# Overlapping the stages of a second block by halves of x, on one core

## The chip, the cores and the metric

One NeuronCore of a Trainium2 chip runs the whole program. The metric is the device time of one execution in microseconds, as a median over runs. All data is float32; weights stream from HBM.

## The reference, cut to what matters

256 tokens with 1024 channels go through two blocks of two layers each. The first block (token mixers and a mixture of experts) is not changed. The second block is, for layer i:

```python
for i in range(2):
    h = h + 0.5 * swiglu(rms_norm(h, ffn1_norm[i]), wg1[i], wu1[i], wd1[i])   # 1024 -> 2816 -> 1024
    hn = rms_norm(h, mix_norm[i])
    h = h + (rglru_mixer(hn, ...) if i == 0 else pool_mixer(hn, w, b, scale))
    h = h + 0.5 * swiglu(rms_norm(h, ffn2_norm[i]), wg2[i], wu2[i], wd2[i])
    gate = sigmoid(rms_norm(h, ple_norm[i]) @ ple_w_gate[i])
    h = h + gate * (p[i] @ ple_w_proj[i])
return rms_norm(h, final_norm)
```

`swiglu(x) = (silu(x @ wg) * (x @ wu)) @ wd`. `rglru_mixer` projects to 2 x 1280 channels, convolves, computes gates, runs a linear recurrence over the tokens, multiplies by a gelu branch and projects back (`lru_out`). `pool_mixer` takes, for each of four groups of 256 channels, trailing means minus the token, a 256 x 256 map, and returns `(y + b) * scale`.

## The kernel before, in words

x lies in SBUF as two token tiles of 128 x 1024. A product in float32 is made of three matmuls on pairs hi + lo (`mm3`, L324 to L326): a weight of 1 MB comes by a DMA that SyncE issues (`raw`, L275), ScalarE rounds it to `hi` (L308) and VectorE subtracts to `lo` (L309), in four pieces of 128 x 512. `halves_of` (L288) hands out a pair and begins the split of the weight that follows. Weights, pairs and large tiles live in 17 slots of 8 KiB a partition; `phase(n)` says how many of them a stage keeps, and loads run ahead as far as the others go (`pump`).

Each stage of the second block begins with `scaled_T` (L401): 16 transposes of x (`tr`, L397), ScalarE's copy times the gain to `Th` (L411), VectorE's remainder `Tl` (L412). The row norm is a factor that comes in after the products, so `rms_col` runs beside them. The stages:

- `ffn` (L1197): 11 chunks of 256 hidden channels. A chunk is 96 matmuls of 256 columns (`fg`, gate and up) and, one chunk later, 24 of 512 columns onto four accumulators (`acc`, `out_mm` L1247). At the end VectorE adds the four accumulators to x (L1245), and only then do the next stage's transposes start.
- `lru` (L1258): ten products `li`, and between them convolution, gates, two groups of five recurrences on VectorE (L1357) whose inputs GpSimd multiplies (L1356), GpSimd's multiplications by the gelu branch (L1366), and five weights `lru_out` onto `acc`.
- `pool` (L1410): a norm of the rows (`xn`, square and a chain of small VectorE operations), 16 products `pu` with the means' matrix, copies `uT`, 16 products `py`. Then VectorE adds the bias (`pt`, L1432), GpSimd multiplies by the scale (L1434), VectorE adds to x (L1436).
- `ple` (L1439): first p's projection, `pp`, 24 matmuls of 512 columns, with a load and a split of its own (`pT`, `pTh`, `pTl`, weight `ple_p`), copied to `pv`; then transposes, four products `pg`, sigmoid, multiplication by `pv`, addition to x. `ple_final` (L1477) is the last one with the final norm.

The order on each engine is made by a scheduler from the program's order and its estimates, and is fixed when the program is built; each engine then works through its own list in order. PSUM has four banks for `ps` and four for `acc` here.

Of the kernel before, what the change touches and what calls it, by code (L numbers as in the profile page):

```python
# [200 lines left out]
def v2(t):  # L201
    return t.rearrange("p (t n) -> p t n", t=2)


# [1 line left out]
class Prog:  # L206
    def __init__(self, tc, A, off, out, order=None, stop=None):
        """order: the weights' tiles as the program asks for them; None to find it (in self.asked)."""
# [12 lines left out]
    def area(self, psum, tmp):  # L221
        """PSUM banks and small tiles by tag, for a part of the program."""
# [17 lines left out]
    # slots of 8 KiB a partition, given out in the order of the program  # L240
# [47 lines left out]
    def halves_of(self, *key):  # L288
        """hi and lo of a weight; those of the weight that follows are begun before this one's products."""
# [38 lines left out]
    def tok_mm(self, bank, aT, w, t, o=None):  # L328
        """bank[:, o or t] = tokens of tile t x 256 columns of w"""
# [7 lines left out]
    def col_mm(self, bank, w, aT, j):  # L337
        """bank[:, j] = columns j of w x 256 tokens"""
# [7 lines left out]
    def rsqrt(self, ss, n, c):  # L346
        """(ss + c)^-1/2 for [128, n]: a first guess from the exponent's half, a step of third order and one of Newton's."""
# [7 lines left out]
        # y (15/8 - 5/4 w + 3/8 w^2), w = x y^2  # L355
# [15 lines left out]
    def rstd(self, xt, junk=None):  # L371
        """1/sqrt(sum over the row + n eps) for both token tiles; sqrt(n) is left to the caller."""
# [17 lines left out]
    def transposed(self, rows, evac, tags=("ps",) * 4):  # L390
        """rows [128, 2, 1024] -> banks [128, 2 channel tiles, 256 tokens] for evac(k0, bank)."""
# [9 lines left out]
    def scaled_T(self, rows, g, alloc=None):  # L401
        """hi, lo of the transposed rows times the gain column."""
# [14 lines left out]
    def rms_col(self, xt):  # L417
        """1/rms of the rows, [128, 2]."""
# [5 lines left out]
    def rms_row(self, col):  # L424
        """the same along the free axis on every partition, [128, 256]."""
# [9 lines left out]
    def ada(self, l, part, tag="ada"):  # L435
        """part: of shift, scale and gate of the first norm (0 to 2) and of the second (3 to 5)."""
# [1179 lines left out]
```

## Time and profile before

| | |
|---|---|
| median of three runs | 2588.95 us (2579.15 to 2589.79) |
| profiled execution | span 2577.8 us, mean granted TensorE clock 0.925 |
| PE busy | 2253.0 us (87%) |
| VectorE (DVE), ScalarE (ACT), GpSimd (POOL) busy | 1121.9, 796.9, 117.4 us |
| HBM read | 663.20 MB, mean 258 GB/s |
| second block | from about 1578 us to the end |

The profile gives the span of the profiled execution from its first to its last instruction; no other time of that execution is shown. A stage that keeps the PE busy for its whole width is limited by the PE, whatever the other engines' shares are; where the PE is idle, the wait that ends last tells what the stage hangs on. The PE clock is given as a share of full speed (2.4 GHz); half of it is the lower level.

### The profile page before, as it was taken

To read this page: it belongs to the slowest core of one execution; us is meant where nothing else is said; L and a number is where in the kernel's file an instruction comes from. 1 tells how busy PE (TensorE), PEld (TensorE's weight loads), DVE (VectorE), ACT (ScalarE), POOL (GpSimd) and SP (SyncE) were. 2 spreads that over 40 slices of the span, in tenths; PEclk is the share of its full clock that TensorE was granted. 3 is DMA by queue.
4 is the path that set the end of the run, shared out by engine and by line. 5 is a ranking of instruction groups with operands and counts; after the bars stand their busy time and mean duration, and the time that the engine had idled before them with its cause. 6 is when DMAs were issued, how large, how long until landed. Compare 5 with 4: busy or idle time off the path is not lost.

```text
span 2577.8 us, 37968 instructions
## 1 busy us (share of the span) xinstructions
PE 2253.0 (87%) x15658; PEld 1601.2 (62%) x15658; DVE 1121.9 (44%) x2582; ACT 796.9 (31%) x1550; POOL 117.4 (5%) x120
## 2 busy tenths in 40 slices
PE   6999998987878799976666668999899999998997
PEld 4876784322222287742222225999889989988997
DVE  4656563111111476520101105557675566556555
ACT  3244443000000235320000003443764455434444
POOL 0100011000000020010000000000400000000000
PEclk9999798999999999996777778999999999999999
DMA  8365145999999923489999999553365544553540
GB/s 359 144 245 208 55 150 219 417 420 420 420 420 419 381 70 114 166 366 420 419 419 419 419 419 370 190 181 125 125 229 189 188 172 176 180 208 135 189 166 19
DMA packets 92797, 666.72 MB, mean 259 GB/s; under 512 B 10304, under 2 KB 10816, under 8 KB 12496
## 3 DMA queue, kind: packets, MB, share of 16 engines
q1 hardware_dynamic: 92624, 664.29, 65.6%
q8 instruction: 123, 2.02, 0.3%
q14 instruction: 50, 0.41, 0.0%
HBM read 663.20 MB, written 1.05 MB: 258 GB/s over the span
## 4 chain that ended last, share of the span: by engine, by line
PE 37%; DMA 16%; DVE 3%; ACT 1%; issue 1%; POOL 0%; ACTq 0%; SPq 0%; DVEq 0%; POOLq 0%
PE fg L324 7%; PE fg L325 7%; PE fg L326 7%; DMA raw<-in_e_down_dram 6%; DMA raw<-in_e_up_dram 5%; DMA raw<-in_e_gate_dram 5%; PE acc L326 3%; PE acc L324 3%; PE acc L325 3%; PE ri L1339 1%; DVE lo L309 1%; PE pg L324 0%; PE pg L325 0%; PE pg L326 0%; PE li L325 0%
## 5 line engine op out<-in xcount | busy, mean ns | idle before, releaser
L308 ACT CAST hi<-raw 128x512 fp32r<-128x512 f32 x748 | 412.1, 617 | 408.7 <-DVE lo L309 186.2
L309 DVE TENSOR_TENSOR lo<-raw,hi 128x512 fp32r<-128x512 f32 x748 | 479.6, 691 | 132.9 <-PE acc L325 53.9
L324 PE MATMUL fg<-Th,hi 128*128 128x256 f32 x1408 | 402.1, 286 | 6.3 <-DVE Tl L412 6.3
L325 PE MATMUL fg<-Th,lo 128*128 128x256 f32 x1408 | 401.2, 285 | 0.0
L326 PE MATMUL fg<-Tl,hi 128*128 128x256 f32 x1408 | 400.7, 285 | 0.0
L1133 PE MATMUL eu<-raw,XG 128*32 128x256 f32 (+1 forms) x1536 | 216.9, 548 | 73.8 <-DMA raw<-in_e_up_dram 73.8
L324 PEld LDWEIGHTS fg<-Th,hi 128*128 128x128 f32 x1408 | 273.3, 194 | 8.5 <-DVE Tl L412 7.1
L325 PEld LDWEIGHTS fg<-Th,lo 128*128 128x128 f32 x1408 | 273.3, 194 | 1.4
L326 PEld LDWEIGHTS fg<-Tl,hi 128*128 128x128 f32 x1408 | 272.9, 194 | 0.0
L1133 PE MATMUL eg<-raw,XG 128*32 128x256 f32 (+1 forms) x1536 | 207.7, 522 | 60.1 <-DMA raw<-in_e_gate_dram 60.0
L1133 PE MATMUL ed<-raw,hTs 128*32 128x256 f32 (+1 forms) x1536 | 209.4, 530 | 52.3 <-DMA raw<-in_e_down_dram 51.8
L1144 DVE TENSOR_TENSOR hid<-sg,eu 128x512 f32<-128x512 f32 (+1 forms) x32 | 17.7, 554 | 514.6 <-issue 335.8
L1133 PEld LDWEIGHTS eu<-raw,XG 128*32 128x32 f32 (+1 forms) x1536 | 69.0, 136 | 216.9 <-DMA raw<-in_e_up_dram 116.8
L1165 DVE TENSOR_TENSOR osb<-ed,g 32x512 f32<-32x512 f32 (+1 forms) x128 | 70.9, 554 | 279.1 <-PE ed L1133 277.5
L1133 PEld LDWEIGHTS eg<-raw,XG 128*32 128x32 f32 (+1 forms) x1536 | 68.2, 133 | 199.6 <-DMA raw<-in_e_gate_dram 98.7
L1133 PEld LDWEIGHTS ed<-raw,hTs 128*32 128x32 f32 (+1 forms) x1536 | 66.0, 133 | 179.7 <-DMA raw<-in_e_down_dram 103.4
L1141 ACT ACTIVATE sg<-eg 128x512 f32<-128x512 f32 (+1 forms) x32 | 15.7, 490 | 507.1 <-PE eg L1133 507.0
L324 PE MATMUL acc<-hi,fhh 128*128 128x512 f32 x352 | 137.4, 390 | 0.0
L325 PE MATMUL acc<-hi,fhl 128*128 128x512 f32 x352 | 137.4, 390 | 0.0
L324 PE MATMUL wi<-hi,hTh 128*128 128x256 f32 x448 | 134.6, 301 | 3.0 <-DVE lo L309 2.2
L326 PE MATMUL acc<-lo,fhh 128*128 128x512 f32 x352 | 136.9, 389 | 0.0
L326 PE MATMUL wi<-lo,hTh 128*128 128x256 f32 x448 | 132.3, 296 | 2.5 <-DVE lo L309 2.4
(319 smaller groups left out, 3415.7 us busy)
## 6 DMA issues: line engine op xcount, KB each, us to landing
raw<-in_e_gate_dram SPq DMA_DIRECT2D x128, 1024.0 KB, 19.9
raw<-in_e_up_dram SPq DMA_DIRECT2D x128, 1024.0 KB, 19.9
raw<-in_e_down_dram SPq DMA_DIRECT2D x128, 1024.0 KB, 19.9
raw<-in_ada_dram SPq DMA_DIRECT2D x48, 1024.0 KB, 6.9
raw<-in_ffn_g_dram SPq DMA_DIRECT2D x44, 1024.0 KB, 4.9
raw<-in_ffn_u_dram SPq DMA_DIRECT2D x44, 1024.0 KB, 4.9
raw<-in_ffn_d_dram SPq DMA_DIRECT2D x44, 1024.0 KB, 4.8
raw<-in_w_in_dram SPq DMA_DIRECT2D x18, 1024.0 KB, 19.9
```

Of the source, the lines that this page charges most:

```text
L308: self.nc.scalar.copy(hi[:, c], src[:, c])
L309: self.nc.vector.tensor_tensor(lo[:, c], src[:, c], hi[:, c].bitcast(F32), ALU.subtract)
L324: mm(out, ah, bh, start=first, stop=False)
L325: mm(out, al, bh, start=False, stop=False)
L326: mm(out, ah, bl, start=False, stop=last)
L1133: nc.tensor.matmul(p[M * c:M * c + M, 0:N], lhs(k), v2(w)[:, kk, c * N:c * N + N], start=k == 0, stop=k == 7, tile_position=(0, M * c))
L1141: nc.scalar.activation(sg[:, 0:N], pg[:, 0:N], AF.Silu)
L1144: nc.vector.tensor_tensor(hid[:, 0:N], sg[:, 0:N], pu[:, 0:N], ALU.mult)
L1165: nc.vector.tensor_tensor(ob[r:r + 32, s, c * N:c * N + N], p[q0:q0 + 32, 0:N], g2[r:r + 32, s, c * N:c * N + N], ALU.mult)
L1339: nc.tensor.matmul(b[:, gi * 256:gi * 256 + 256], wt, xc[BLOCKS[n][0]], start=q == 0, stop=q == len(ids) - 1)
```

## The change

The transposed halves of x become a class `Turn`, made two channel tiles at a time by `turn(k0)`, in banks of the `acc` tag. `out_mm` finishes the accumulators of the first 512 channels before those of the second; in the last chunk `between` adds them to x at once, and the next stage's `turn(0)` and `turn(2)` are placed in the middle of the second half. The first products of a stage are made for two weights, on channel tiles 0 to 3 first, then `turn(4)`, `turn(6)`, then tiles 4 to 7. The norm's column waits behind those copies. The pool's scale is multiplied into bias and weights on GpSimd, the bias is added to x on GpSimd, and VectorE adds `py` to x out of PSUM. The projection of p becomes `ple_values`, run as a filler in `lru` (ahead of the last gelu) and in `pool` (between norm and `pu`); `pv` is kept through the second feed-forward, so `phase` is 10 there instead of 9 (12 instead of 11 in `lru`). In the first block only the order of the last combine's four additions changes.

```diff
+class Turn:
+    def turn(self, k0):
...
+        b = p.ps("tr", "acc")
+        xv = v2(p.x)
+        for kk in range(2):
+            for t in range(2):
+                nc.tensor.transpose(b[:, kk * 256 + t * 128:kk * 256 + t * 128 + 128],
+                                    xv[:, t, (k0 + kk) * 128:(k0 + kk + 1) * 128], p.con("ident"))
+        for kk in range(2):
+            k = k0 + kk
+            s, g = b[:, kk * 256:kk * 256 + 256], self.gain[:, k:k + 1]
+            self.act = nc.scalar.activation(self.hi(k), s, AF.Copy, scale=g)
+            self.dve = nc.vector.scalar_tensor_tensor(self.lo(k), s, g, self.hi(k).bitcast(F32), ALU.mult, ALU.subtract)
...
+    def out_mm(self, acc, w, a, first, last, between=None):
+        wh, wl = w
+        for d in range(2):
+            for j, (ah, al) in enumerate(a):
+                for t in range(2):
+                    o = t * 128
+                    q = j * 1024 + d * 512
+                    self.mm3(acc[d][t], ah[:, o:o + 128], al[:, o:o + 128], wh[:, q:q + 512], wl[:, q:q + 512],
+                             first and j == 0, last and j == 1)
+                if between is not None:
+                    between(d, j)
+
+    def residual(self, acc, add, nxt):
+        def between(d, j):
+            if j == 1:
+                for t in range(2):
+                    add(acc[d][t], v2(self.x)[:, t, d * 512:d * 512 + 512], t)
+            if nxt is not None and (d, j) == (1, 0):
+                nxt.turn(0)
+                nxt.turn(2)
+        return between
...
+            ws = [self.halves_of(f"ffn{n}_{m}", i, c) for m in "gu"]
+            bs = [self.ps("fg") for _ in "gu"]
+            T.turn(0)
+            T.turn(2)
+            for b, w in zip(bs, ws):
+                for j in range(2):
+                    if b is bs[1] and j == 1:
+                        T.turn(4)
+                        T.turn(6)
+                    self.col_part(b, w, T, (j,), range(4))
+            for b, w in zip(bs, ws):
+                self.col_part(b, w, T, (0, 1), range(4, 8))
+                self.free(*w)
+                yield b
...
             if c == 0:
-                col = self.rms_col(self.x)
+                with self.behind(T.act), self.behind(T.dve):
+                    col = self.rms_col(self.x)
...
         scan(range(5, NT))
         branch(4)
+        filler()
         gelu(2, 3, 4)
         out(range(4, NT))
...
-    def pool(self):
+    def pool(self, nxt, filler):
         nc = self.nc
-        xn = self.norm_rows(self.x)
...
+        filler()
         mw, pw, brt = self.weight("k_pool"), self.weight("pool_w"), self.weight("brow2")
         br = v2(brt)
+
+        nc.gpsimd.tensor_tensor(br[:, 0], br[:, 0], br[:, 1], ALU.mult)
+        pws = self.big("pws")
+        for gi in range(4):
+            s = br[:, 1, gi * 256:gi * 256 + 256].unsqueeze(1).to_broadcast([128, 2, 256])
+            p2 = lambda a: a[:, gi * 512:gi * 512 + 512].rearrange("p (c n) -> p c n", c=2)
+            nc.gpsimd.tensor_tensor(p2(pws), p2(pw), s, ALU.mult)
...
+            xs = v2(self.x)[:, :, gi * 256:gi * 256 + 256]
+            nc.gpsimd.tensor_tensor(xs, xs, br[:, 0, gi * 256:gi * 256 + 256].unsqueeze(1).to_broadcast([128, 2, 256]), ALU.add)
...
-            tv = self.t2("pt").rearrange("p (t n) -> p t n", t=2)
-            o = gi * 256
-            nc.vector.tensor_tensor(tv, b.rearrange("p (t n) -> p t n", t=2),
-                                    br[:, 0, o:o + 256].unsqueeze(1).to_broadcast([128, 2, 256]), ALU.add)
-            nc.gpsimd.tensor_tensor(tv, tv, br[:, 1, o:o + 256].unsqueeze(1).to_broadcast([128, 2, 256]), ALU.mult)
-            xs = v2(self.x)[:, :, o:o + 256]
-            nc.vector.tensor_tensor(xs, xs, tv, ALU.add)
-        self.free(xn, mw, pw, brt, uTt)
-
-    def ple(self, i):
+            xs = v2(self.x)[:, :, gi * 256:gi * 256 + 256]
+            nc.vector.tensor_tensor(xs, xs, b.rearrange("p (t n) -> p t n", t=2), ALU.add)
+
+        means(0)
+        for gi in range(4):
+            if gi < 3:
+                means(gi + 1)
+            mapped(gi)
+            if gi:
+                nxt.turn(2 * gi - 2)
+        self.free(xn, mw, pw, brt, uTt, pws)
+
+    def ple_values(self, i):
...
+            if nxt is not None and n > 1:
+                nxt.turn(2 * n - 4)
             yield n
-        self.free(*hT, pvt)
...
+        self.free(self.pv)
+        if nxt is not None:
+            nxt.turn(4)
```

How this moves instructions shows at three places. The rows name line, operation, output, inputs and shape; a count stands behind rows that follow each other.

VectorE at the start of the second block's first feed-forward, from the last combine's additions (`x<-x,cb`) on. Before:

```order
L1176 TENSOR_TENSOR x<-x,cb 128x512
L309 TENSOR_TENSOR lo<-raw,hi 128x512
L1176 TENSOR_TENSOR x<-x,cb 128x512 x3
L309 TENSOR_TENSOR lo<-raw,hi 128x512 x3
L412 SCALAR_TENSOR_TENSOR Tl<-tr,cols,Th 128x256 x7
L309 TENSOR_TENSOR lo<-raw,hi 128x512 x2
L412 SCALAR_TENSOR_TENSOR Tl<-tr,cols,Th 128x256
L309 TENSOR_TENSOR lo<-raw,hi 128x512 x6
```

Now:

```order
L1212 TENSOR_TENSOR x<-x,cb 128x512
L345 TENSOR_TENSOR lo<-raw,hi 128x512
L1212 TENSOR_TENSOR x<-x,cb 128x512 x3
L345 TENSOR_TENSOR lo<-raw,hi 128x512 x11
L238 SCALAR_TENSOR_TENSOR T<-tr,cols,T 128x256 x8
L414 SCALAR_TENSOR_TENSOR junk,ss<-x 128x1024
```

Eight more splits, of the second and the third weight, stand ahead of the transposed halves.

VectorE in the recurrent stage, from the second group of five recurrences (`lf<-lf`, x5 before and x1, x4 now) to the additions of the output product. Before:

```order
L1357 SCALAR_TENSOR_TENSOR lf<-lf 128x256 x5
L309 TENSOR_TENSOR lo<-raw,hi 128x512 x3
L1315 TENSOR_TENSOR lf<-li,rrow 128x256 x2
L309 TENSOR_TENSOR ly<-lf,ly 128x256 x6
L309 TENSOR_TENSOR lo<-raw,hi 128x512 x28
```

Now:

```order
L1456 SCALAR_TENSOR_TENSOR lf<-lf 128x256
L1452 SCALAR_TENSOR_TENSOR lf<-q,lf 128x256
L1456 SCALAR_TENSOR_TENSOR lf<-lf 128x256 x4
L345 TENSOR_TENSOR lo<-raw,hi 128x512 x4
L1414 TENSOR_TENSOR lf<-li,rrow 128x256 x2
L345 TENSOR_TENSOR pTl<-pT,pTh 128x512
L345 TENSOR_TENSOR lo<-raw,hi 128x512 x4
L345 TENSOR_TENSOR ly<-lf,ly 128x256 x6
L345 TENSOR_TENSOR lo<-raw,hi 128x512 x28
```

The first four `lo` are now those of `ple_p`, the next four those of the first `lru_out` weight, of which the first piece stood ahead of the recurrences before.

The PE in the pool stage, from `pu` to the first gate product. Before:

```order
L326 MATMUL acc<-lo,fhh 128x512
L1420 MATMUL pu<-raw,xn 128x256 x16
L1428 MATMUL py<-raw,uT 128x256 x16
L397 MATMUL tr<-k_early,x 128x128 x16
L324 MATMUL fg<-Th,hi 128x256
```

Now:

```order
L362 MATMUL pp<-lo,pTh 128x512
L1546 MATMUL pu<-raw,xn 128x256 x8
L1557 MATMUL py<-pws,uT 128x256 x4
L1546 MATMUL pu<-raw,xn 128x256 x4
L1557 MATMUL py<-pws,uT 128x256 x4
L232 MATMUL tr<-k_early,x 128x128 x4
L1546 MATMUL pu<-raw,xn 128x256 x4
L1557 MATMUL py<-pws,uT 128x256 x4
L232 MATMUL tr<-k_early,x 128x128 x4
L1557 MATMUL py<-pws,uT 128x256 x4
L232 MATMUL tr<-k_early,x 128x128 x4
```

The row ahead of `pu` is the last of 24 `pp` now; the means, the maps and the transposes are interleaved, and the last four transposes follow 36 `fg`.

## Rows read from the trace of the kernel before

**Rows 1.** Busy time by stretch: window, width, busy (records) of five engines, clock, DMA.

```profile
1600.00:1765.00 165.00, 165.00 (x1170) 155.73 (x1169) 91.29 (x148) 74.12 (x133) 0.10 (x1) 1.00 0.53 186
```

**Rows 2.** What the PE waits for from 1578 us on: total, times, longest.

```profile
PE fg L324 <- DVE Tl L412: 6.3, 3, 2.3
PE pu L1420 <- issue: 5.5, 1, 5.5
PE acc L326 <- DVE lo L309: 5.0, 1, 5.0
PE li L325 <- DVE lo L309: 4.9, 1, 4.9
...
PE pg L324 <- DVE Tl L412: 3.3, 2, 1.7
```

**Rows 3.** Timeline, pool stage: start, duration, engine, operation, count, idle time before.

```profile
2322.21 8.75 PE L1420 MATMUL pu<-raw,xn 128*128 128x256 f32 x32 [5.54 <-issue]
2330.80 7.07 PE L1428 MATMUL py<-raw,uT 128*128 128x256 f32 x32
2337.71 0.60 PE L397 MATMUL tr<-k_early,x 128*128 128x128 f32 x4
...
2344.72 0.57 PE L324 MATMUL fg<-Th,hi 128*128 128x256 f32 x1
...
2348.72 0.41 PE L325 MATMUL fg<-Th,lo 128*128 128x256 f32 x1
2348.93 0.41 PE L326 MATMUL fg<-Tl,hi 128*128 128x256 f32 x1
...
2349.61 0.28 PE L325 MATMUL fg<-Th,lo 128*128 128x256 f32 x1
2349.73 0.28 PE L326 MATMUL fg<-Tl,hi 128*128 128x256 f32 x1
...
2337.53 2.49 POOL L1434 TENSOR_TENSOR pt<-pt,raw 128x512 f32<-128x512 f32 x2 [1.90 <-DVE pt L1432]
```

**Rows 4.** Timeline, second recurrent wait, on PE, VectorE and GpSimd.

```profile
1863.34 0.40 PE L324 MATMUL acc<-hi,ly 128*128 128x512 f32 x1
...
1864.95 0.39 PE L325 MATMUL acc<-hi,ly 128*128 128x512 f32 x1
1870.36 0.80 PE L326 MATMUL acc<-lo,ly 128*128 128x512 f32 x1 [5.01 <-DVE lo L309]
...
1862.59 5.51 DVE L1357 TENSOR_TENSOR_SCAN lf<-lf 128x256 f32<-128x256 f32 x5 [0.63 <-POOL lf L1356]
1868.03 3.40 DVE L309 TENSOR_TENSOR lo<-raw,hi 128x512 fp32r<-128x512 f32 x3
1871.36 0.74 DVE L1315 TENSOR_TENSOR lf<-li,rrow 128x256 f32<-128x256 f32 x2
...
1866.46 4.43 POOL L1366 TENSOR_TENSOR lf<-lf 128x256 f32<-128x256 f32 x4
```

**Rows 5.** Timeline, start of the second block's first feed-forward.

```profile
1579.95 1.89 DVE L309 TENSOR_TENSOR lo<-raw,hi 128x512 fp32r<-128x512 f32 x3
1581.76 3.01 DVE L412 SCALAR_TENSOR_TENSOR Tl<-tr,cols,Th 128x256 fp32r<-128x256 f32 x7
...
1583.46 0.39 PE L324 MATMUL fg<-Th,hi 128*128 128x256 f32 x1 [2.26 <-DVE Tl L412]
```

**Rows 6.** Timeline, VectorE within a feed-forward loop, GpSimd idle.

```profile
2006.80 2.49 DVE L309 TENSOR_TENSOR lo<-raw,hi 128x512 fp32r<-128x512 f32 x4
```

**Rows 7.** Busy time by stretch at three seams, columns as in Rows 1.

```profile
1772.20:1778.00 5.80, 4.28 (x31) 3.50 (x30) 5.71 (x13) 5.56 (x14) 0.30 (x3) 1.00 0.01 1
...
1898.00:1907.00 9.00, 7.14 (x48) 6.87 (x47) 7.12 (x25) 4.17 (x10) 0.00 (x0) 0.81 0.81 321
...
2122.00:2132.00 10.00, 7.32 (x46) 6.42 (x46) 8.36 (x19) 10.00 (x24) 0.00 (x0) 0.83 0.31 105
```

**Rows 8.** The page's list of DMA issues: count, KB each, us to landing.

```profile
raw<-in_ffn_g_dram SPq DMA_DIRECT2D x44, 1024.0 KB, 4.9
```

More of the change, by code (lines that the diff above doesn't have):

```diff
@@ L1194, in moe, with turner, col_part @@
         self.free(gwb, g2b)
-    def ffn(self, i, n):
+    def turner(self, gain):
+        return Turn(self, gain)
+    def col_part(self, bank, w, T, js, ks):
+        wh, wl = [v8(a) for a in w]
+        mm = self.nc.tensor.matmul
+        for j in js:
+            o = bank[:, j * 256:j * 256 + 256]
+            for k in ks:
+                h, l = T.hi(k), T.lo(k)
+                c = slice(j * 128, j * 128 + 128)
+                mm(o, wh[:, k, c], h, start=k == 0 and j == 0, stop=False, skip_group_check=True)
+                mm(o, wh[:, k, c], l, start=False, stop=False, skip_group_check=True)
+                mm(o, wl[:, k, c], h, start=False, stop=k == 7, skip_group_check=True)
@@ new lines, in tok_part @@
+    def tok_part(self, bank, w, T, t, ks):
+        wh, wl = [v8(a) for a in w]
+        mm = self.nc.tensor.matmul
+        o = bank[:, t * 256:t * 256 + 256]
+        c = slice(t * 128, t * 128 + 128)
+        for k in ks:
+            h, l = T.hi(k)[:, c], T.lo(k)[:, c]
+            mm(o, h, wh[:, k, :], start=k == 0 and t == 0, stop=False, skip_group_check=True)
+            mm(o, l, wh[:, k, :], start=False, stop=False, skip_group_check=True)
+            mm(o, h, wl[:, k, :], start=False, stop=k == 7, skip_group_check=True)
@@ new lines, in accumulators @@
+    def accumulators(self):
+        return [[self.ps("acc", "acc") for _ in range(2)] for _ in range(2)]
+    def out_mm(self, acc, w, a, first, last, between=None):
[9 more added lines that the diff above has]
+                    between(d, j)
@@ L1240, in ffn, with lru @@
         down(NC - 1, prev)
-        self.free(*hT)
-        for d in range(2):
-            for t in range(2):
-                xs = v2(self.x)[:, t, d * 512:d * 512 + 512]
-                nc.vector.scalar_tensor_tensor(xs, acc[t][d], rms["half"][:, t:t + 1], xs, ALU.mult, ALU.add)
-    def out_mm(self, acc, w, a, first, last):
-        wh, wl = w
-        for d in range(2):
-            for j, (ah, al) in enumerate(a):
-                for t in range(2):
-                    o = t * 128
-                    q = j * 1024 + d * 512
-                    self.mm3(acc[t][d], ah[:, o:o + 128], al[:, o:o + 128], wh[:, q:q + 512], wl[:, q:q + 512],
-                             first and j == 0, last and j == 1)
-    def lru(self):
+    def lru(self, T, nxt, filler):
         nc = self.nc
@@ L1296, in product @@
             b = self.ps("li")
-            for j in range(2):
-                self.col_mm(b, w, hT, j)
+            self.col_part(b, w, T, (0, 1), range(8))
             self.free(*w)
@@ L1367, in out @@
                 self.halves(yh[m], yl[m], mu[m])
-        banks = [product(5)]
-        col = self.rms_col(self.x)
-        banks.append(product(6))
+        ws = [self.halves_of("lru_in", c) for c in (5, 6)]
+        banks = [self.ps("li") for _ in range(2)]
+        T.turn(0)
+        T.turn(2)
+        for b, w in zip(banks, ws):
+            for j in range(2):
+                if b is banks[1] and j == 1:
+                    T.turn(4)
+                    T.turn(6)
+                self.col_part(b, w, T, (j,), range(4))
+        for b, w in zip(banks, ws):
+            self.col_part(b, w, T, (0, 1), range(4, 8))
+            self.free(*w)
+        with self.behind(T.act), self.behind(T.dve):
+            col = self.rms_col(self.x)
         row = self.rms_row(col)
@@ L1414, in pool, with means @@
         uT = v8(uTt)
-        for gi in range(4):
+        def means(gi):
             b = self.ps("pu")
@@ L1485, in ple_final @@
         s8 = self.small(8, "s8").rearrange("p (t n) -> p t n", t=2)
-        for n in self.ple(i):
+        for n in self.ple(i, T, None):
             c = slice(n * 256, n * 256 + 256)
```

141 lines of the change are left out of this document (99 added, 42 removed).

## The prediction, made before the changed kernel ran

> **What bounds the kernel now.** I read the busy time by stretches first. In the feed-forward loops the PE column equals the width of the stretch, 165 us of 165 at a clock of 1.00 [rows 1]: there the PE is the limit, and the diff leaves the number of its matmuls as it was. So the second block can win only at the seams between stages. The waits of the PE say what ends last there [rows 2]: `fg` waits for `Tl`, VectorE's half of the transposed x, three times for 6.3 us together; `pu` sits 5.5 us with nothing named (the pool's norm); `pg` waits 3.3 us in two places; and in the recurrent stage `li` and `acc` wait 4.9 and 5.0 us for VectorE's `lo` of a weight. That is 25 us. The timelines around the seams then show a second cost: after such a wait the granted clock falls to the lower of its two levels (1.2 for 2.4 GHz), and matmuls that take 0.12 us are issued every 0.21 us for a while (2348.72 to 2348.93 against 2349.61 to 2349.73) [rows 3]. Both are small beside a span of 2577.8 us: 0.5% is about 13 us, and about what a measurement of this kernel can tell from no change. All of this is priced against the profiled execution; its span lies 11 us below the median 2588.95 of the three runs, and I subtract the same sum from that median.
>
> **The change part by part.** Signs are times added. A 24-matmul group of 512 columns (a chunk's `acc`, or all of `pp`) is 24 x 0.23 = 5.5 us, from the eight `acc` issued between 1863.34 and 1864.95 [rows 4].
>
> *First feed-forward (1580 us): +3.7.* The early transposes cannot help, since the stage ahead of it has no half-wise product. But the first products now ask for two weights before the transposes, and asking splits the next weight too: VectorE's order has eleven `lo` ahead of the first T, where there were three. They start at 1579.95 [rows 5]; at 0.62 us each (2.49 for four, undisturbed) [rows 6] they end at 1586.8, and the first T, 3.01 / 7 = 0.43 us [rows 5], at 1587.2. The first `fg` stood at 1583.46. Nothing on the PE is left to cover it: the 16 transposes are done by then. Bounds: 3.5 at the 0.60 of the three of before (1.81 us from their start to the first `Tl`), 5 if the longer wait keeps the clock low for longer.
>
> *First feed-forward to recurrence: -1.2.* From 1772.2 to 1778 the PE is busy 4.28 of 5.80 us at full clock [rows 7], so 1.5 us is to be had. Now eight transposes stand between the last `acc`, with six `acc` (1.4 us) behind them to cover the copies. I leave 0.3; bounds 0 and -1.5.
>
> *First recurrent wait: +0.5.* One `lo` that ran ahead of the recurrences now runs behind them (1.13 each there [rows 4], against six matmuls of 0.12).
>
> *Second recurrent wait: +9.4.* The ple's projection is put here as a filler. It should run while the PE waits for the recurrences, but on VectorE its four `lo` and `pTl` stand behind the five recurrences as well, and `lo` of lru_out's first weight behind them. The recurrences end at 1868.1. There three `lo` took 3.40 us, 1.13 each, while GpSimd ran its multiplications until 1870.9 [rows 4]; at rest a `lo` is 0.62 [rows 6]. Three at 1.13 and one at 0.62 end at 1872.1, the two `lf` (0.74) at 1872.8, `pTl` at 1873.4. Only four `pp` run before that. Then 20 `pp` and 24 `acc` follow, 10.1 us, to 1883.5; before, `acc` went on at 1870.36 with 16 of its 24 left, to 1874.1. Of the difference, 9.4, the 5.5 of `pp` is work that leaves the ple; 3.9 is loss. With every `lo` at 0.62 it would be 7.9. The lower clock after the wait costs about the same in both.
> The Trainium skill (SBUF — State Buffer, Who interferes with whom) says that a VectorE instruction with two SBUF inputs contends with a GpSimd instruction that reads SBUF, and one with a single SBUF input does not. The 1.13 against 0.62 agrees. By that rule the filler is placed badly, and the sum is 1.5 us worse than by undisturbed splits.
>
> *Recurrence to second feed-forward: -3.1.* From 1898 to 1907 the PE is busy 7.14 of 9.00 us, 1.9 idle; a clock of 0.81 means 3.4 us at the lower level, where 0.12 of each 0.21 us is work, so 1.5 more [rows 7]. Same cure as above; I leave 0.3. Bounds 0 and -3.4.
>
> *To the first ple: -7.1.* The 24 `pp` are gone (5.5), and half of `pg`'s 3.3 us of waits (1.6) [rows 2].
>
> *Ple to feed-forward of layer 1: -3.6.* From 2122 to 2132: 2.7 idle, and 0.83 is 3.4 us at the lower clock, 1.5 [rows 7]: 4.2. Two pairs are now turned behind quarters 2 and 3 and only the last behind the last quarter, for which I leave 0.6.
>
> *Pool stage: -7.5.* Before, the PE stops at 2322.21 - 5.54 = 2316.7 and starts `fg` at 2344.72, slowly until 2349.4: 22 matmuls, and the other 74 of its first 96 at 0.12 end at 2358.3 [rows 3]. After: `pp` takes 5.5 us of the norm's wait and keeps the PE at work, to 2322.2, when xn is there. 16 `pu` and 16 `py` at 7.07 / 16 = 0.44 us are 14.1, 16 transposes 4 x 0.60, 96 `fg` 11.5 [rows 3], to 2350.2; and 0.6 for the last T, which VectorE does behind six `lo`. The old chain `pt`, GpSimd, x is off the path: GpSimd scales the pool's weights during the last `acc` chunk (four at 2.49 / 2 us, 5 us [rows 3], from the slot that the chunk before frees at about 2311) and adds the bias behind xn, while VectorE has `uT` and the adds from PSUM. Without that cover it would cost those 5 us.
>
> *To the last ple: -7.1*, as with the first: 5.5 and 1.6. The tail is unchanged.
>
> Sum: 3.7 - 1.2 + 0.5 + 9.4 - 3.1 - 7.1 - 3.6 - 7.5 - 7.1 = -16.0: a span of 2561.8, and **2573.0** against the median.
>
> **Rivals.**
> *Given back.* The T of the second half stand behind four to eight `lo` at each seam. If at four of them (the recurrence, the second feed-forward, the first ple, the pool) a group of four, 2.5 us [rows 6], ends last on the PE's path, 10 us return: -6, or 2583, no change that can be told. For it: VectorE ends almost every wait in rows 2. Against: by then 36 matmuls (4.3 us) are queued ahead.
> *More.* If the waits close wholly (another 1.2), the filler's splits are early enough to fill the recurrent wait (3.9) and the first seam loses nothing (3.7): -25, or 2564. Against: the orders of VectorE below.
> *GpSimd in the way.* If the slot for the scaled weights comes late, the four scalings (5 us) fall into the pool's norm, hold up its square and its chain, and `py` waits for them: -11, or 2578. The skill's section named above gives the mechanism; the doubled `lo` [rows 4] show it. Against: VectorE is idle of splits then.
> *Slower.* The projected values keep a slot through both second feed-forwards, so one weight fewer is loaded ahead. These loops have 66 weights; a load takes 4.9 us to land [rows 8] against 5.7 us of PE per weight (a chunk has 120 matmuls and three weights, so the 1170 of 165 us are 29 weights [rows 1]). If the loads became the limit and each weight came x late, the gain is gone at x = 16 / 66 = 0.24 us and the kernel is slower by over 0.5% from 0.44 us; at 0.6 us it is +24, or 2613. For it: the slots alone set when a load starts. Against: the DMA share there is 0.53, and several loads are under way.
> *That it does not do what it says:* in part that holds, the filler being the case; it is in the sum.
>
> **How the numbers follow.** Forecast 0.56, given back 0.20, more 0.10, GpSimd 0.08, slower 0.06. The forecast's own bounds (the filler 7.9 to 9.4, seams at 0 or at all their idle time) give -24 to -10, mostly beyond -13: I count 0.47 of its 0.56 as faster. With "more" and half of GpSimd's 0.08 that is 0.61; same 0.33; slower 0.06. The range reaches from "more", 25 us down, with the 10 us by which the shown runs differ partly counted, to just short of no change: 2557 to 2585.
>
> **What would show it.** Right: `fg` of the first feed-forward starts 3 to 4 us later with eleven `lo` ahead; the wait of `pg`, `pu` and of `tr` for x is gone; `pp` ahead of lru_out starts after 1873 by the old clock of that stage, and the wait there is longer than 5.0 us; at 2316 `pp` fills the norm and no matmul there runs at the lower level. Wrong: `fg` waits within the loops, a wait for `lo` at the second-half products, or `pp` running inside the recurrences.

## The result, and the profile after

| | before | changed kernel |
|---|---|---|
| median, first comparison (4 runs each) | 2585.36 us | 2558.22 us (2554.98 to 2561.46) |
| ratio of the medians | | 0.9889 [0.9863, 0.9916] |
| median, second comparison (11 and 6 runs) | 2580.82 us | 2557.08 us |
| ratio | | 0.9898 [0.9874, 0.9922] |
| profiled execution | span 2577.8 us, clock 0.925 | span 2558.4 us, clock 0.922 |
| PE, VectorE, ScalarE, GpSimd busy | 2253.0, 1121.9, 796.9, 117.4 us | 2258.8, 1117.6, 799.0, 123.1 us |

The change is faster by 1.1%. The forecast was -16.0 us, a ratio of 0.9938, which lies outside both intervals; 2558 us lies inside the stated range.

To see where the gain came from I cut the second block at landmarks that both kernels have: the first transposes, the norm's row product `rb` of each following stage, the second group of gate products `ri`, and the last weight's first `pg`. In the timeline of the PE of the changed kernel they are (start, duration, engine, operation, count):

```profile
1581.82 1.93 PE L232 MATMUL tr<-k_early,x 128*128 128x128 f32 x16
1602.90 0.60 PE L464 MATMUL rb<-k_early,rc 128*128 128x128 f32 x4
1792.88 0.66 PE L464 MATMUL rb<-k_early,rc 128*128 128x128 f32 x4
1845.35 1.03 PE L1438 MATMUL ri<-lf,raw 128*128 128x256 f32 x4
1923.12 0.60 PE L464 MATMUL rb<-k_early,rc 128*128 128x128 f32 x4
2137.41 0.60 PE L464 MATMUL rb<-k_early,rc 128*128 128x128 f32 x4
2346.19 0.68 PE L464 MATMUL rb<-k_early,rc 128*128 128x128 f32 x4
2546.70 0.28 PE L1259 MATMUL pg<-lo,T 128*128 128x256 f32 x1
```

In the kernel before the same starts are 1579.24, 1596.55, 1787.86, 1840.60, 1914.88, 2140.82, 2358.36 and 2566.09 us. The differences between them give the stretches, in us, beside the terms of the prediction:

| stretch | before | after | measured | forecast |
|---|---|---|---|---|
| A: first transposes to `rb` of the first feed-forward | 17.31 | 21.09 | +3.8 | +3.7 |
| B: to `rb` of the recurrent stage | 191.31 | 189.98 | -1.3 | -1.2 |
| C1: to the second `ri` (first recurrent wait) | 52.74 | 52.46 | -0.3 | +0.5 |
| C2: to `rb` of the second feed-forward (second recurrent wait +9.4, seam -3.1) | 74.28 | 77.78 | +3.5 | +6.3 |
| D: to `rb` of layer 1 (ple -7.1, seam -3.6) | 225.93 | 214.29 | -11.6 | -10.7 |
| E: to `rb` behind the pool | 217.54 | 208.77 | -8.8 | -7.5 |
| F: to the last `pg` | 207.73 | 200.51 | -7.2 | -7.1 |
| all of the second block, with its tail | 998.60 | 976.54 | -22.1 | -16.0 |

The signs are right everywhere but in C1. Of the 6.1 us between forecast and measurement C2 carries 2.8, E 1.3, D 0.9 and C1 0.8.

The waits of the PE in the second block answer to [rows 2] (who waited, for whom: total, times, longest):

```profile
PE fg L1246 <- DVE T L238: 5.8, 1, 5.8
PE pp L360 <- ACT pTh L344: 3.9, 1, 3.9
PE li L1247 <- DVE lo L345: 3.4, 1, 3.4
PE pp L360 <- DVE lf L1414: 1.1, 1, 1.1
```

Of three `fg` waits one is left, and it is longer; `pu` and `pg` no longer wait; `acc` waits no more, but `pp` does, twice. The busy time by stretches answers to [rows 7] for the seams and shows the pool's norm and the recurrent wait (window, width, busy of PE, PEld, VectorE, ScalarE, GpSimd, clock, DMA share, GB/s):

```profile
1872.00:1882.00 10.00, 8.81 (x22) 6.34 (x23) 5.79 (x10) 5.43 (x13) 4.83 (x6) 0.57 0.03 12
1907.00:1916.00 9.00, 9.00 (x66) 8.38 (x65) 4.51 (x9) 2.18 (x5) 0.00 (x0) 1.00 0.78 294
2123.00:2133.00 10.00, 9.93 (x83) 9.65 (x82) 7.78 (x17) 8.32 (x18) 0.00 (x0) 1.00 0.31 107
2313.00:2323.00 10.00, 10.00 (x47) 8.32 (x46) 5.63 (x19) 7.34 (x13) 4.48 (x5) 1.00 0.84 314
```

The last three rows are two seams (ahead of the second feed-forward and of layer 1) and the pool's norm: the PE is busy in all of their time but 0.07 us, and its clock is 1.00. In the recurrent stage (first row) it is 0.57, so 8.6 of the 10 us lie at the lower level, and the PE has just waited 3.9 us.

*The first feed-forward.* The timeline of VectorE and the PE there, which answers to [rows 5]:

```profile
1582.62 6.71 DVE L345 TENSOR_TENSOR lo<-raw,hi 128x512 fp32r<-128x512 f32 x11
1589.24 2.84 DVE L238 SCALAR_TENSOR_TENSOR T<-tr,cols,T 128x256 fp32r<-128x256 f32 x7
1589.78 0.58 PE L1246 MATMUL fg<-T,hi 128*128 128x256 f32 x1 [5.79 <-DVE T L238]
```

Eleven `lo`, 0.61 each, stand ahead of the first T, as forecast. Two `fg` that need ScalarE's half alone run at 1583.50; the third waits for the first T, until 1589.78.

*The recurrent stage*, timeline of VectorE, GpSimd, ScalarE and the PE (answers to [rows 4]):

```profile
1836.51 4.07 DVE L345 TENSOR_TENSOR lo<-raw,hi 128x512 fp32r<-128x512 f32 x4
1837.01 4.17 POOL L1465 TENSOR_TENSOR lf<-lf 128x256 f32<-128x256 f32 x4 [2.13 <-ACT lf L1421]
...
1861.32 0.83 DVE L1451 TENSOR_TENSOR q<-lf 128x256 f32<-128x256 f32 x2 [1.05 <-ACT lf L1421]
...
1865.79 1.22 DVE L1456 TENSOR_TENSOR_SCAN lf<-lf 128x256 f32<-128x256 f32 x1 [0.63 <-POOL lf L1455]
...
1867.75 3.45 DVE L1456 TENSOR_TENSOR_SCAN lf<-lf 128x256 f32<-128x256 f32 x4
1871.12 3.00 DVE L345 TENSOR_TENSOR lo<-raw,hi 128x512 fp32r<-128x512 f32 x4
1874.70 0.68 DVE L345 TENSOR_TENSOR pTl<-pT,pTh 128x512 fp32r<-128x512 f32 x1
...
1871.63 0.74 POOL L1465 TENSOR_TENSOR lf<-lf 128x256 f32<-128x256 f32 x1 [2.14 <-ACT lf L1421]
1876.73 3.72 POOL L1465 TENSOR_TENSOR lf<-lf 128x256 f32<-128x256 f32 x4 [4.36 <-ACT lf L1421]
...
1869.84 1.28 ACT L1421 ACT_TABLE_LOAD   x1
1871.13 0.42 ACT L1421 ACTIVATE lf<-lf 128x256 f32<-128x256 f32 x1
1871.45 0.60 ACT L344 CAST pTh<-pT 128x512 fp32r<-128x512 f32 x1
...
1872.11 1.65 PE L360 MATMUL pp<-hi,pTh 128*128 128x512 f32 x3 [3.87 <-ACT pTh L344]
1874.84 0.80 PE L360 MATMUL pp<-hi,pTh 128*128 128x512 f32 x1 [1.08 <-DVE lf L1414]
1882.49 0.39 PE L360 MATMUL acc<-hi,ly 128*128 128x512 f32 x1
```

The filler fills little, as forecast: four `pp` start before `pTl` is done at 1875.38, and 20 after. Those take (1882.49 - 1875.38) / 20 = 0.36 us each instead of 0.23. In the pool (timeline, answers to [rows 3]) the first `pu` start at 2318.54, right behind `pp`, and GpSimd has both of its jobs beside other work:

```profile
2318.54 3.69 PE L1546 MATMUL pu<-raw,xn 128*128 128x256 f32 x16
2307.96 5.49 POOL L1536 TENSOR_TENSOR pws<-raw 128x512 f32<-128x512 f32 x4 [26.23 <-PE acc L362]
2318.97 4.96 POOL L1551 TENSOR_TENSOR x<-x,raw 128x512 f32<-128x512 f32 x4 [5.52 <-ACT xn L1526]
```

### The profile page after: what moved, and what is told of

Same layout as the page of the kernel before. It is cut to its first block, busy times and chain, and to the rows that moved or that the text cites. A ratio compares the mean times of both kernels' runs of the same rounds, so it can differ in the third digit from the quotient of the medians.

```text
span 2558.4 us, 38009 instructions
## 1 busy us (share of the span) xinstructions
PE 2258.8 (88%) x15658; PEld 1603.6 (63%) x15658; DVE 1117.6 (44%) x2578; ACT 799.0 (31%) x1551; POOL 123.1 (5%) x125
## 5 line engine op out<-in xcount | busy, mean ns | idle before, releaser
L345 DVE TENSOR_TENSOR lo<-raw,hi 128x512 fp32r<-128x512 f32 x748 | 487.1, 694 | 348.9 <-issue 129.5
L1246 PE MATMUL fg<-T,hi 128*128 128x256 f32 x1408 | 399.4, 284 | 5.9 <-DVE T L238 5.8
L1247 PE MATMUL fg<-T,lo 128*128 128x256 f32 x1408 | 398.9, 284 | 0.0
L1245 PE MATMUL fg<-T,hi 128*128 128x256 f32 x1408 | 398.7, 284 | 0.0
L1246 PEld LDWEIGHTS fg<-T,hi 128*128 128x128 f32 x1408 | 270.9, 192 | 8.1 <-DVE T L238 6.5
L1245 PEld LDWEIGHTS fg<-T,hi 128*128 128x128 f32 x1408 | 270.4, 192 | 1.5
L1247 PEld LDWEIGHTS fg<-T,lo 128*128 128x128 f32 x1408 | 270.9, 192 | 0.0
L1169 PE MATMUL eg<-raw,XG 128*32 128x256 f32 (+1 forms) x1536 | 213.1, 540 | 54.2 <-DMA raw<-in_e_gate_dram 54.1
L1169 PEld LDWEIGHTS eg<-raw,XG 128*32 128x32 f32 (+1 forms) x1536 | 69.6, 136 | 196.7 <-DMA raw<-in_e_gate_dram 95.3
```

The source lines that it names most:

```text
L345: self.nc.vector.tensor_tensor(lo[:, c], src[:, c], hi[:, c].bitcast(F32), ALU.subtract)
L1169: nc.tensor.matmul(p[M * c:M * c + M, 0:N], lhs(k), v2(w)[:, kk, c * N:c * N + N], start=k == 0, stop=k == 7, tile_position=(0, M * c))
L1245: mm(o, wh[:, k, c], h, start=k == 0 and j == 0, stop=False, skip_group_check=True)
L1246: mm(o, wh[:, k, c], l, start=False, stop=False, skip_group_check=True)
L1247: mm(o, wl[:, k, c], h, start=False, stop=k == 7, skip_group_check=True)
```

## The experiments

My theory after the result: each term is a local price, so that the order of VectorE's list makes the loss in A and most of that in C2, while the filler in the pool and the halves (the early transposes and the split first products) make the gain in D, E and F. Rivals: the loss in A is the price of the half-wise products themselves; the filler in the recurrent stage pays even so; and a part of the gain is the first block's. In all runs below the changed kernel is the base, and the stretches of its table are what is compared; between two executions of it (the last run of this section) they repeat within 0.1 us. Stretches that aren't named moved by less than 0.8 us (A by 0.6 in a run whose edit lies behind it). Each run of this section was profiled once.

**The first transposes ahead of the weights' splits** (before `ws = ...` in the first products of `ffn`)

```diff
+            if not T.done:
+                for k0 in range(0, 8, 2):
+                    T.turn(k0)
             ws = [self.halves_of(f"ffn{n}_{m}", i, c) for m in "gu"]
```

> The first feed-forward asks for its transposes before it asks for its two weights; VectorE then has three splits ahead of the transposed halves instead of eleven. Theory (order of VectorE's list): the stretch from the block's first transposes to the norm-row product, 17.3 us before and 21.1 us in the changed kernel, returns to 17 to 17.6 us, everything behind it is unchanged, and the span is 3.8 us shorter. Rival (the second weight's splits are needed soon after, so that the wait only moves): 19 to 21 us.

Measured: A 15.1 us, 6.0 less than in the changed kernel and 2.2 less than before; 17 to 17.6 were expected, and what gives the 2.2 no run isolates. Three `lo` stand ahead of the first T again (timeline of this kernel):

```profile
1582.03 1.89 DVE L345 TENSOR_TENSOR lo<-raw,hi 128x512 fp32r<-128x512 f32 x3
1583.83 2.83 DVE L238 SCALAR_TENSOR_TENSOR T<-tr,cols,T 128x256 fp32r<-128x256 f32 x7
1584.36 0.38 PE L1246 MATMUL fg<-T,hi 128*128 128x256 f32 x1 [0.85 <-DVE T L238]
```

The products are by halves as before, so it is VectorE's order alone that costs: shown.

**The projection of p back in the first ple**

```diff
+        if i == 0:
+            self.ple_values(0)
         pv = v2(self.pv)
...
-                        self.lru(then, T, lambda: self.ple_values(0))
+                        self.lru(then, T, lambda: None)
```

> The projection of p of layer 0 is put back at the start of the ple instead of filling the recurrent stage. Theory (the filler fills nothing there, and its splits and the wait for its own operands cost 2 to 4 us): from the recurrence's norm-row product to that of the second feed-forward 130.2 us falls to 121 to 123, by more than the 5.5 us of the products, and the stretch with the ple rises from 214.3 to about 220; net 2 to 4 us shorter. Rival (the filler does fill the wait): net 2 us or more longer.

C2 69.6 (-8.2), C1 -1.2, D 219.6 (+5.35); B, E and F as in the changed kernel. Net -4.4 without A (2 to 4 were expected): the filler as placed costs more than it fills. Of the 4.4, 1.2 lie in C1, ahead of the filler's place, and stay unexplained. The 5.35 is `pp` with its 24 matmuls at 0.23, back on the path.

**The same in the pool** (`i == 1`, and `self.pool(T, lambda: None)`)

> The projection of p of layer 1 is put back at the start of the last ple. Theory (there it covers the pool's norm and keeps the clock up): the stretch with the pool, 208.8 us, falls by its 5.5 us of products and rises by the wait of 5.5 and by 1.5 to 2 us of lower clock, to about 210.5; the last stretch rises from 200.5 to about 206; net 6 to 8 us longer. Rival (the norm hides behind something else by now): net 0 to 2 us.

E +7.1 and F +5.3, 12.3 together, where 6 to 8 were expected: the sign was right, the size was not. F's 5.3 is `pp` back on the path. Waits of the PE of this kernel:

```profile
PE pu L1546 <- issue: 6.2, 1, 6.2
PE py L1557 <- ACT uT L1548: 2.6, 1, 2.6
```

and its stretch at the norm (columns as above):

```profile
2306.00:2330.00 24.00, 15.22 (x52) 11.92 (x51) 9.90 (x25) 9.45 (x17) 7.50 (x6) 0.80 0.33 131
```

The norm's wait comes back, longer than the 5.5 us of [rows 2], a second one (`py` for `uT`) with it, and a part of the rest runs at the lower clock: 0.80 of 24 us means 9.6 us at the lower level. The two waits add 8.8 us and `pp` takes its 5.5 out of E, which makes 3.3 of the 7.1; the other 3.8 or so fit the lower clock, an estimate from these rows. The same filler thus pays 12.3 us here and costs 4.4 there. One difference is what its splits stand behind; further runs below test that.

**Without the two transposes in the last chunk**

```diff
-            if nxt is not None and (d, j) == (1, 0):
-                nxt.turn(0)
-                nxt.turn(2)
```

> No transposes within the output products; x is still added by halves, and the next stage's transposes are asked for with its first products. Theory (early transposes are what closes the seams): about 1.3, 3.1, 1.6 and 1.6 us return at the four seams behind an output product (recurrence, second feed-forward of layer 0, first and last ple), 6 to 8 us in all. Rival (adding x by halves and splitting the first products already closes them): 0 to 2 us in all.

B +4.4, D +1.9, 5.6 in all where 6 to 8 were expected, and otherwise spread: of the 3.1 expected at the second feed-forward (C2) and the 1.6 at the last ple (F) nothing came in C2 and 0.2 in F. So the early transposes close the seams in B and D; those of C2 and F stay closed without them. In B the wait moves to the T of the first products; waits of the PE there (1770 to 1800 us):

```profile
PE li L1246 <- DVE T L238: 2.3, 2, 1.8
PE li L1245 <- ACT T L237: 0.8, 1, 0.8
```

**First products not split by halves** (in `ffn`, `lru` and `ple` all four `turn` first, then `col_part` or `tok_part` once, over `range(8)`)

```diff
-            for b, w in zip(bs, ws):
-                self.col_part(b, w, T, (0, 1), range(4, 8))
+            for b, w in zip(bs, ws):
+                self.col_part(b, w, T, (0, 1), range(8))
```

> All transposes of a stage are asked for ahead of its first products, which take all eight channel tiles of one weight at a time. Theory (the split of the products is what hides the second half's copies): 1 to 2 us return at each of the recurrence, the second feed-forward of layer 0 and the two ples, and as much at the pool, 5 to 9 us in all; the first feed-forward does not change. Rival (the early transposes close the seams alone): 0 to 2 us in all.

B +2.2, D +1.0, E +1.9, 4.9 in all, just under the 5 to 9 expected; C2 (-0.1) and F (+0.2) again don't move. A +0.5: taking the split away does not bring its loss back, so the half-wise products as such cost nothing there.

**Both of these**

> Neither transposes within the output products nor split first products: x is still added by halves. Theory (either of the two hides a part that the other hides too, so that only both missing shows the whole): the stretches with the recurrence, the second feed-forward and the two ples return to within 1 us of the kernel before (191.3, and for the ples 214.3 + 3.4 and 200.5 + 1.6), with the recurrence at 194 as without early transposes; 9 to 14 us in all above the changed kernel. Rival (they add simply): 6.3 of the one and 4.9 of the other, 11 us, with no stretch above the sum of the two.

B +4.4, D +2.6, E +3.5, 10.3 in all. B came to 194.4 as expected, but C2 (77.8) and F (200.7) did not return. In B the split products are worth 2.2 us where the early transposes are there and nothing where they aren't.

In E, +3.5 is more than the sum of the two (-0.3 and +1.9), yet the two do not cover for each other there: the early transposes that this run takes away lie in no seam of E, as those in front of the second feed-forward of layer 1 are asked for by the pool. Without the halves alone and without both, the same `fg` waits for the same T, 1.73 and 1.74 us; then the 58 `fg` up to `rb` run at a clock of 1.00 in the one and of 0.81 in the other. Timeline of the PE and busy time by stretches (columns as above), first without the halves, then without both:

```profile
2355.64 0.39 PE L1246 MATMUL fg<-T,hi 128*128 128x256 f32 x1 [1.73 <-DVE T L238]
2355.64:2362.99 7.35, 7.33 (x58) 7.13 (x59) 5.88 (x20) 4.17 (x8) 0.00 (x0) 1.00 0.29 88
...
2342.17 0.39 PE L1246 MATMUL fg<-T,hi 128*128 128x256 f32 x1 [1.74 <-DVE T L238]
2342.17:2351.01 8.84, 8.82 (x58) 8.62 (x59) 5.87 (x20) 4.41 (x9) 0.00 (x0) 0.81 0.23 68
```

The 1.5 us between +1.9 and +3.5 are that clock; why it fell in one and not in the other, no run shows.

C2's seam stays closed in all three runs, and so does most of F's. What else the change does there, adding x by halves and the altered order of VectorE, was not undone in any run; it is the rival that is left, and the early transposes are not shown to be what closes these two.

**The pool's chain as it was** (bias on VectorE, scale on GpSimd, addition on VectorE; unscaled weights)

> The pool's bias, scale and addition go back to VectorE, GpSimd, VectorE per group of channels (pt), in the changed kernel's interleaved order. Theory (that chain stood on the path before each group's transposes): the stretch with the pool, 208.8 us, becomes 211 to 214 us. Rival (the interleaving alone hides the chain): 208.5 to 209.5 us.

E +2.45, as expected, with a wait of the transposes for `x` of 1.2 us. So of E's 8.8 us the filler holds about 7 and the scale in the weights about 2.5; with the halves' 1.9 that is more than 8.8, so these parts overlap.

Against the whole, the runs so far give 12.3 (filler in the pool), 10.3 (early transposes and split products), 2.5 (the pool's scale), less 4.4 (filler in the recurrent stage) and 3.8 (A): 16.9 of 22.1 us, if they add up. The other 5 or so lie with parts that no run took away: x added by halves, and the transposes behind the quarters of the ple and in the pool.

**GpSimd's multiplication by the gelu branch on VectorE**, to see whether it makes the `lo` slow

```diff
-                nc.gpsimd.tensor_tensor(mu[m], ig[m], gg[m], ALU.mult)
+                nc.vector.tensor_tensor(mu[m], ig[m], gg[m], ALU.mult)
```

> The multiplication by the gelu branch in the recurrent stage goes from GpSimd to VectorE (the rest as in the changed kernel). Theory (a split waits while GpSimd multiplies): the four splits behind the first recurrences, 4.07 us, take 2.4 to 2.7 us, and those behind the second, 3.00 us, the same; the stretches of the stage hardly move, since VectorE has nine short multiplications more. Rival (those splits are slow for another reason, such as their scalar engine halves coming late): 3.6 us or more.

In the changed kernel four `lo` behind the first recurrences took 4.07 us (at 1836.51) beside four GpSimd multiplications, and the four behind the second 3.00 with one of them. With the multiplications moved (timeline of VectorE):

```profile
1833.65 2.46 DVE L345 TENSOR_TENSOR lo<-raw,hi 128x512 fp32r<-128x512 f32 x4
1868.32 2.47 DVE L345 TENSOR_TENSOR lo<-raw,hi 128x512 fp32r<-128x512 f32 x4
```

Both are at the 0.62 of rest. So the slow splits are GpSimd's doing, shown by taking it away. The Trainium skill (SBUF — State Buffer, Who interferes with whom), cited in the prediction, agrees. (For an instruction with a single SBUF input that section excepts VectorE's two-port modes, which the prediction left out; nothing here rests on it.) No stretch moved by more than 0.4 us (C2 77.5); VectorE now has the multiplications to do itself. The mechanism is real, and moving them gains nothing.

**Filler with its splits ahead of the recurrences** (`scan` first starts the waiting split; p is loaded at the start of `lru` and split before the second recurrences)

```diff
         def scan(ms):
+            if self.ready and len(self.pairs) < 2:
+                self.begin(*self.ready[0][0])
...
         branch(3)
+        self.ple_split()
         scan(range(5, NT))
```

> Recurrent stage: ahead of each group of recurrences one more weight is split, and p is loaded at the stage's start and split ahead of the second group, so that splits no longer stand behind the recurrences on VectorE. Theory (the order of VectorE's list makes both waits): the wait of li (3.4 us, and 2.6 us of lower clock behind it) goes, the projection runs while the second recurrences run; the two stretches of the stage, 52.5 and 77.8 us, become 47 to 49 and 70 to 73 us. Rival (the waits are set by the recurrences' own results or by slots and loads): each within 1.5 us of the changed kernel, or longer.

C1 46.3 (-6.2, a little more than expected) and C2 74.8 (-3.0), a miss: expected for C2 were 70 to 73. Timeline of VectorE and the PE:

```profile
1853.73 0.68 DVE L345 TENSOR_TENSOR pTs<-pT,pTs 128x512 fp32r<-128x512 f32 x1
1855.38 5.52 DVE L1458 TENSOR_TENSOR_SCAN lf<-lf 128x256 f32<-128x256 f32 x5 [0.64 <-POOL lf L1457]
1853.93 0.63 PE L360 MATMUL pp<-hi,pTs 128*128 128x512 f32 x2
1861.60 0.50 PE L360 MATMUL pp<-hi,pTs 128*128 128x512 f32 x1 [3.17 <-DVE lf L1415]
```

`pp` now starts before the recurrences and runs beside them, and then waits 3.2 us all the same: for a bank of PSUM that VectorE frees by an addition (`lf`, L1415) which stands behind the recurrences. So one wait of VectorE's list was behind another.

**First transposes and filler together**

> fill together with the transposes asked for first in the first feed-forward. Theory (the two are separate places of VectorE's list): the gains add, the second block is 6 us shorter than that of fill, about 960 us against 976.5 in the changed kernel. Rival: less than 5 us of the 6.

A 15.2, C1 46.3, C2 74.7, the second block 961.0: the changed kernel's 976.5 less 5.9 and 9.7. The two gains add.

**Together, with `pp` in the banks of `acc`**

```diff
-                b = self.ps("pp")
+                b = self.ps("pp", "acc" if i == 0 else "ps")
```

> The first transposes asked for first, the recurrent stage's splits ahead of the recurrences, and the projection of layer 0 in the accumulators' banks, so that it needs no bank that waits for a copy behind the recurrences. Theory (the 3.2 us that the projection still waited came from that bank): the stretch from the second gate products to the second feed-forward's norm-row product, 74.7 us, becomes 70 to 72, the second block 956 to 959 us, and the time 17 to 21 us below the changed kernel. Rival (lru_out's first split, behind the recurrences, sets the end there): 74 us or more, as with the look before.

A miss: C2 78.75, 4 us more. Now `acc` waits for the banks (timeline of the PE, ScalarE and VectorE):

```profile
1868.29 0.79 PE L360 MATMUL acc<-hi,ly 128*128 128x512 f32 x1 [6.99 <-ACT pv L1601]
1867.65 2.05 ACT L1601 COPY pv<-pp 128x512 f32<-128x512 f32 x4 [3.83 <-DVE lo L345]
1862.99 4.57 DVE L345 TENSOR_TENSOR lo<-raw,hi 128x512 fp32r<-128x512 f32 x4
```

The copies `pv` that free them start on ScalarE only when the four `lo` behind the recurrences are done on VectorE; what in those `lo` they need, the trace does not say. The median was 2546.13 (6 runs), ratio 0.9847 [0.9819, 0.9875] to the kernel before.

**Together, timed; and the same without a filler in the recurrent stage**

> The kernel of best_look, timed: splits ahead of the recurrences, projection of layer 0 as filler, first transposes asked for first. Theory (second block 15.5 us shorter than the changed kernel's, first block unchanged): 35 to 40 us below the kernel before, ratio 0.9845 to 0.9865. Rival (the shorter second block is given back): ratio above 0.988.

> As best_timed, but the projection of layer 0 back at the start of its ple; one more split still stands ahead of each group of recurrences. It tells what the filler itself is worth once VectorE's list no longer delays it. If the filler now fills a wait that is otherwise idle, this kernel's second block is 3 to 6 us longer than best_timed's 961. If the wait had only moved to the copies and banks behind the recurrences, it is within 1.5 us of 961, or shorter.

With the filler: 2542.81 (6 runs), ratio to the kernel before 0.9846 [0.9818, 0.9874], second block 960.8. With `pp` back in the ple and the other two edits kept: 2546.41, ratio 0.9865 [0.9842, 0.9888], C2 71.7, D 219.65, second block 963.2. Once its splits come first, the filler is worth 2.4 us, between the two expectations (3 to 6, and 1.5 or less); as the change places it, it costs 4.4. So the place of the splits decides the sign, but 2.4 is not the 12.3 of the pool: the wait for a bank (3.2 us above) stays. The first of the two beats both kernels: its second block is 38 us shorter than before's, against 22 for the change.

**The change once more**

> The changed kernel unchanged, to tell how much of its gain lies in the second block. Theory (the change shortens only the second block, by 22.1 us as the two traces have it; what the first timing shows beyond is the first block's spread): the difference of the medians is 19 to 25 us, and the second block lasts 976 to 977 us again. Rival (the first block also gained): 27 us or more.

2557.08 us against 2580.82, a difference of 23.7, and the second block 976.6 us again: the theory's ranges. The changed kernel's block is thus the same twice within 0.1 us; the 998.6 of the kernel before come from its one profiled execution. The two executions of the changed kernel differ by 7.8 us in span (2558.4 and 2550.6) and by 7.9 in where the second block starts (1581.8 and 1573.9), so that their difference lies ahead of it. Over all 15 profiled executions of versions of the change, whose edits all lie in the second block, that start lies anywhere from 1573.9 to 1593.9 us; the kernel before has 1579.2. A gain of 22.1 us is a ratio of 0.9915, which lies in both intervals. So the differences of the medians, 27 and 24 us, fit 22 and that scatter; that the first block gained nothing is not shown more closely than the intervals allow.

## Why the prediction was right in its places and wrong in its size

*Right.* The first feed-forward's loss (+3.8 for +3.7) by its own mechanism, which the first experiment took away; the sign named for it, a first `fg` 3 to 4 us later, holds from the third `fg` on (7.96 us behind the first transpose, for 4.57 before), as two now run early. The last ple (-7.2 for -7.1): `pp` is 5.3 of it, but the other 1.9 are not shown to be the early transposes'. The seam before the recurrence (-1.3 for -1.2) is in part luck: without the early transposes B is 194.4, 3.1 longer than before, so that the changed order of the first products costs something there that the prediction did not have. The filler in the recurrent stage as a loss beyond the 5.5 us that it moves, in sign: undoing it gave 4.4 us back (its size is the next point). `pp` fills the norm, with the clock at 1.00. The slow loads of the rival *slower* show nowhere: no `fg` waits within the loops.

*Wrong: the second recurrent wait, +9.4.* This is the term that missed by most. Measured apart from the seam: before, the transposes behind the 120 `acc` start 57.40 us behind the second `ri` (1898.00). After, the 25th `acc` is issued at 1887.93, 42.58 behind `ri`; before at 1876.23, 35.63 behind it; from there both run at 0.23 each. So this term is +6.95, below its low bound of 7.9, and the seam keeps +3.50 - 6.95 = -3.45 for a forecast of -3.1 (a number that came true without its cause being shown: C2 does not move when the early transposes go). The step that failed is "the recurrences end at 1868.1 ... three `lo` at 1.13 and one at 0.62 end at 1872.1 ... `pTl` at 1873.4". On the clock of before (4.75 us less) the recurrences ended at 1871.12 - 4.75 = 1866.4, 1.7 earlier: the first `q` of their chain started 0.6 earlier (1861.32 - 4.75 = 1856.6, for 1857.19 before), one `lo`, 0.6, had moved from ahead of them to behind, and the multiplications and the recurrences took 0.4 less. The four `lo` took 3.00, not 4.0, since of GpSimd's multiplications only one fell beside them; the next four moved behind, to 1876.73. `pTl` ended at 1875.38 - 4.75 = 1870.6, 2.8 before its time. I had carried a price from a row of before (1.13 beside GpSimd) to a place where the change had moved GpSimd's work away, and its start from a list of VectorE whose order the change had altered: both were to be read from the order of the changed kernel. A smaller error goes against it: the lower clock after the wait cost 2.45 us here (from `pTl`'s end to the 25th `acc` 12.55, not the 10.1 of 44 matmuls at full clock) and 2.1 before (1876.2, not 1874.1), so "about the same" was 0.35 short. 9.4 - 2.8 + 0.35 = 6.95.

The check that "`pp` starts after 1873 and the wait is longer than 5.0 us" failed with it: it starts at 1872.11 - 4.75 = 1867.4 after 3.9 us. The wait is named for ScalarE's `pTh`; on its list too the filler stood behind an activation and a table load (1869.84 to 1871.45). The prediction had read VectorE's list only.

*Wrong: the rests that I left at each seam.* D came out 0.9 better and E 1.3 better. In D I had left 0.6 us for the last pair of transposes, and the seam is closed (9.93 of 10.00 busy). In E the 0.6 that I added for the last T wasn't needed, and the 16 transposes hold the PE for 1.6 us, not 2.4: a row of four shows 0.60, but the next instruction starts 0.36 to 0.44 after it. (The 16 `pu` and 16 `py` of the program stand as 32 records each in the trace, at 0.22; their total, 13.9 for 14.1, was right.) Those rests were caution without a row behind them, all of one sign; so was C1's 0.5, where C1 came out at -0.3 with its wait at 3.4 us for 4.9. C2 (2.8), D, E and C1 (0.8) make up 5.8 of the 6.1 us between -16.0 and -22.1.

*And the base.* I subtracted from 2588.95, a median of three runs with 10 us between them. Over more runs it is 2580.8 to 2585.4. The sum against the span, 2561.8, missed the span of 2558.4 by 3.4 us, and that by luck: the second block of that execution starts 2.6 us later than before's, which hides a part of the 6.1. The number against the median missed by 15.

*The rivals.* *Given back* fell: no group of four `lo` ended last at a seam but the first. *More* named two of the right conditions: earlier splits for the filler and nothing lost in the first seam are what the last kernels do. They gain 38 us in all where it said 25; the 6.2 us of C1, the first recurrent wait, it did not name. *GpSimd in the way* has its mechanism (the slow splits), at no cost in the pool: the scalings ran from 2308 to 2313.5, under the last `acc`. *Slower* fell too, as said.

## What to carry to other kernels

A filler only fills a wait if everything it needs, its operands' splits, its loads and its banks, is ahead of that wait on every in-order list, not only on the engine that is idle: read each such list before pricing it, and read it in the changed order. The same edit gave 12.3 us in one stage and cost 4.4 in another, and moving five small splits (with p's load) turned the loss into a gain of 2.4. And compare stretches between landmarks rather than medians when an early, noisy part of the program moves the end by as much as the change is worth.

## What the runs showed of the hardware that I had not expected

A split `lo` of 128x512 on VectorE took 0.62 us at rest and about 1.0 beside GpSimd's multiplications of 128x256 (4.07 for four), and moving those off GpSimd brought the four to 2.46. In the recurrent stage the PE waited 3.9 us, and the 10 us from there on, with a second wait of 1.1 us, had a mean clock of 0.57; the lower clock cost 2.45 us on top of the waits. Two runs with the same wait of 1.7 us for the same T had a clock of 1.00 and of 0.81 behind it, so the length of a wait alone did not tell what it would cost. Where `pp` filled a wait (the pool's norm, PE busy 10.00 of 10.00) the clock stayed at 1.00; without it waits of 6.2 and 2.6 us stood there at a mean clock of 0.80, and the filler returned 12.3 us. The end of the first block lay anywhere in 20 us over 15 executions whose edits lie behind it.
